# Entry products of a hybrid decoder block: where the weight sums are made, and when

## The chip, the cores and the metric

One Trainium2 chip, one of its cores. The metric is the device time of one execution in microseconds (us). A kernel is run several times and the median is given; one more execution is recorded by the hardware profiler, and all times of single instructions come from that one. TensorE (PE) multiplies matrices and loads their weights (PEld), VectorE (DVE) and ScalarE (ACT) work on elements, GpSimd (POOL) does so too and issues DMAs from its own queue, SyncE (SP) issues most DMAs. Each engine runs its instructions strictly in order.

## What is computed

A decoder block on one sequence of 1024 tokens with 1024 channels. The input is normed, scaled and shifted by a conditioning vector, which gives h. One large product `h @ w_in` yields the queries, keys, values and gates of a retention layer (4 heads), the queries, keys and values of dilated attention (3 groups of 4 heads), and two branch gates. The rest (retention by chunks of 128 tokens, attention, a squared-ReLU MLP) follows. Cut to what matters here:

```
h = modulate(rms_norm(x, g), sh1, sc1)
proj = h @ w_in
parts = jnp.split(proj, IN_OFFSETS, axis=-1)
rq, rk, rv, rg = parts[0], parts[1], parts[2], parts[3]
aq, ak, av = parts[4 + 3 * gi], parts[5 + 3 * gi], parts[6 + 3 * gi]
```

The change is in how the attention values `av` (and some of the retention values `rv`) are got from h. All operands and results are float32.

## The kernel before, in words

**Products.** Each float32 operand is split into a high and a low part, `hi` by a ScalarE cast and `lo` by a VectorE subtraction, and one product is three matmuls, `mm3` at L207 (low weights), L209 (low moving data) and L211 (both high); the names on a matmul line show what is multiplied. A block product of 2 x 2 blocks is done with seven block products in place of eight (a scheme of Strassen's kind). It needs sums of weight blocks, `s1` = 21 + 22, `s2` = s1 + 11, `s4` = s2 + 12 and `s3` = 21 + 11, where "21" names a block of the weight, and sums of blocks of h, called t1, t2, t3 and t4.

**Order.** The part around the change is written out by hand: the order in the program text is the order on each engine. Tiles come from pools with a few buffers per tag: `wraw` (three, for raw weights), `whl` (three each of "wh" and "wl"), `x4` (26, for anything of 128 x 1024). When a tile is placed in a buffer that an earlier tile used, its first instruction waits for the last use of that one. [...]

**Steps.** `first_values` (L800) makes plain values. `more_values` (L1012), called the entry below, runs eleven products i = 0 to 10 in the order of `USEQ`: four of the retention values (11, 11, 12, 12 for two halves), then seven of the attention values: 11, 12, s1, s2, s4, s3, 22. Each product has four parts p = 0 to 3 of twelve matmuls of 128 x 512, 48 in all, and its result is taken out of PSUM one part later by `u_post` (L956). `queries_keys` (L1209), called the pair stage, then runs 18 pairs of weight halves with the class `Blocks`, and after it `values` (L1329) makes the rest of the retention values. Then come the retention chunks, `chunk` (L690), and the rest of the block.

**Weights of the entry.** `u_load` (L911) loads the two raw tiles `ur` of product i from SP. For the products s1, s2 and s3 it loads block "21"; `u_add` (L924) then adds the other blocks by accumulating DMAs from POOL's queue (L931): one block on s1, two on s2, two more on s1's tile to make s4, one on s3, each for two tiles, 12 transfers in all of 512 KB. `u_w` (L933) makes `uwh` by ScalarE (L937) and queues the subtraction for `uwl` on VectorE (L940, L942). For product i + 1 it is called at p = 2 and 3 of product i. In between, an if/elif ladder places the scaling and splitting of h (`h_scale`, `h_split`) and its sums (`sums_of_h`, L1102).

**Around it.** `shift_out` (L1001) multiplies the plain values' correction, copies it to the tile `shw` and adds it to the stored values `vad` by four accumulating DMAs from POOL (L1010). `bias_out` (L445) stores three rows and spreads each by four broadcasts. `a_load` (L1145) loads the raw weights of a pair; those of pair 0 are loaded in product 9, those of pair 1 at the start of `queries_keys`. In `values`, `v_base` (L1321) loads the tile `vm` from DRAM and copies it into PSUM as the start value of `va`. At the end of `values`, three state tiles are made (L1367 to L1369), and with `chunk_tiles` before them they take over SBUF that the value products used. The first chunk's tile `sm` is written at L650, `state` at L737.

Of the kernel before, what the change touches and what calls it, by code (L numbers as in the profile page):

```python
# [11 lines left out]
F32 = mybir.dt.float32  # L12
# [5 lines left out]
P = 128  # L18
# [6 lines left out]
DV = 512  # L25
# [115 lines left out]
def block_kernel(ctx, tc, io, stop=None, dbg=None):  # L141
# [3 lines left out]
    def fv(t):  # L145
        return t.bitcast(F32)
# [246 lines left out]
    def bias_cut(t, g):  # L393

        return t[0][:, 384 * g:384 * g + 384] if g < 2 else t[1][:, :384]
# [42 lines left out]
    def bias_rows(g):  # L438
# [3 lines left out]
        r = bias_cut(rows, g)[:12]  # L442
        nc.scalar.copy(r, ps)

    def bias_out(g):  # L445

        nc.sync.dma_start(brow_d[g], bias_cut(rows, g)[:12])
# [459 lines left out]
    def u_block(i, blk, j):  # L907
        s, b = USEQ[i][0], ("11", "12", "21", "22").index(blk)
        return io["w_av2"][b, j] if s == "av" else io["w_rv"][b, 2 * int(s[1]) + j]

    def u_load(i):  # L911

        n = USEQ[i][1]
        for j in range(2):
            if i in (1, 7):
                t = x4(f"ur{i}{j}")
            elif i in (3, 5, 9):
                t = whl.tile([P, 1024], F32, tag=("wh", "wl")[j], name=f"ur{i}{j}")
            else:
                t = wraw.tile([P, 1024], F32, tag="raw", name=f"ur{i}{j}")  # L920
            U["raw", i, j] = t
            nc.sync.dma_start(t, u_block(i, "21" if n[0] == "s" else n, j))

    def u_add(i):  # L924

        n = USEQ[i][1]
        for blk in {"s1": ("22",), "s2": ("22", "11"), "s4": ("11", "12"), "s3": ("11",)}[n]:
            for j in range(2):
                if n == "s4":
                    U["raw", i, j] = U["raw", i - 2, j]  # L930
                nc.gpsimd.dma_start(U["raw", i, j], u_block(i, blk, j), accum_op=ALU.add, max_dma_last_dim=8192)  # L931

    def u_w(i, j):  # L933
# [3 lines left out]
        nc.scalar.activation(hi, src, AF.Copy, scale=sign)  # L937
        U["w", i, j] = hi, lo
        if sign > 0:
            late_low(lambda: nc.vector.tensor_sub(lo, src, fv(hi)))  # L940
        else:
            late_low(lambda: nc.vector.scalar_tensor_tensor(lo, src, -1.0, fv(hi), op0=ALU.mult, op1=ALU.subtract))  # L942
# [69 lines left out]
    def more_values(ahead):  # L1012

        last = len(USEQ) - 1
        post = []

        def ready(*fs):
            for f, *args in fs:
                f(*args)

        for i, (s, n) in enumerate(USEQ):
            if i in (0, 1, 2, 3, 8):
                u_load(i + 2)
            for k in {4: (6, 7), 5: (9,), 6: (8,)}.get(i, ()):
                if k != 8:
                    u_load(k)
                u_add(k)
            if i == 0:
                for m in range(4):
                    for p in range(4):  # L1030
                        u_mm(0, p, [m])
                u_w(1, 0)
                u_w(1, 1)
                for m in range(4):
                    shift_mod(2 * m + 1)
                late_low()
                for m in range(4):
                    shift_rows(2 * m)
                post = [(0, p) for p in range(4)]
                sh = mods[:, SH1:SH1 + NK].rearrange("p (m j) -> p m j", j=2)  # L1040
                nc.vector.tensor_sub(dsh1, sh[:, :, 0], sh[:, :, 1])
                continue
            for p in range(4):
                u_mm(i, p)
                while post:
                    u_post(*post.pop(0))
                post.append((i, p))
                if i == 1:
                    h_scale(2 * p + 1, 0)
                    h_split(2 * p + 1, 0)  # L1050
                elif i == 2:
                    h_scale(2 * p, 1)
                    shift_rows(2 * p + 1)
                elif i == 3:
                    sums_of_h("t1", [p])
                elif i == 4:
                    h_scale(2 * p + 1, 1)
                elif i == 5:
                    sums_of_h("t2", [p])
                elif i == 6:  # L1060
                    h_split(2 * p + 1, 1)
                    sums_of_h("t4s", [p])
                elif i == 7:
                    h_split(2 * p, 1)
                    sums_of_h("t3", [p - 1] if 0 < p < 3 else [2, 3] if p else [])
                elif i == 8:
                    if p == 0:
                        for m in range(4):
                            nc.sync.dma_start(h12_d[m][:, 0], fv(hh[2 * m][:, 512:]))
                            nc.sync.dma_start(h12_d[m][:, 1], fv(hl[2 * m][:, 512:]))  # L1070
                    if p > 0:
                        sums_of_h("t4", [p - 1])
                elif i == 9:
                    if p == 0:
                        sums_of_h("t4", [3])
                        nc.sync.dma_start(cs, io["cossin"])
                    if p == 1:
                        late_low()
                        a_load(0, 1)
                        a_load(0, 2)  # L1080
                elif i == last:
                    BA.prep((0, ORDER[p]))
                if i < last and p > 1:
                    u_w(i + 1, p - 2)
                    if p == 3:
                        late_low()
                if i == 2 and p == 3:
                    for g in range(3):
                        bias_out(g)
                if i == last and p == 0:  # L1090
                    shift_out()
        BA.flush()
        u_post(*post.pop())

# [112 lines left out]
    BA = Blocks("qa", XA, ["x"] * 4 + ["wh", "wl"] * 3, lambda kind: True, a_place, a_two, a_temps, a_out)  # L1207

    def queries_keys(ahead):  # L1209
        a_load(1, 1)  # L1210
        a_load(1, 2)
# [36 lines left out]

# [71 lines left out]

    def v_base(hp, p):  # L1321

        if p % 2 == 0:
            V["m", hp] = x4(f"vm{hp}{p}")
            nc.sync.dma_start(V["m", hp].rearrange("p (a b) -> p a b", a=2), m11_d[hp][:, p:p + 2])
        V["ps", "a", p] = ps_s(f"va{hp}{p}")
        nc.scalar.copy(V["ps", "a", p], V["m", hp][:, 512 * (p % 2):512 * (p % 2) + 512])

    def values(ahead):  # L1329
        last = len(VSEQ) - 1  # L1330
        for i, (hp, n) in enumerate(VSEQ):
            if i + 2 <= last:
                v_load(i + 2)
            for p in range(4):
                v_mm(i, p)
                if V["post"]:
                    v_post(*V["post"].pop())
                V["post"].append((i, p))
                if n == "s1" and p > 0:
                    v_base(hp, p - 1)  # L1340
                if n == "s2" and p == 0:
# [1452 lines left out]
```

## Time and profile before

| | us |
|---|---|
| runs | 2224.27, 2223.49, 2220.73 |
| median | 2223.49 |
| the profiled execution's own time | 2221.88 |
| its span, first to last instruction | 2220.1 |

TensorE's share of busy time is 98%, VectorE's 67%, ScalarE's 42%, POOL's 8%. The entry lies from 59 to 206 us, the pair stage behind it, the value products end near 671 us, and the first chunk follows.

How to read it. A timeline line has the start in us, the duration in us, the engine, the line of the kernel, the operation, output <- inputs, the shape, and in brackets the idle time of that engine just before and what ended it. Durations of matmuls overlap, so the time that one takes is the distance from its start to the next one's. In the view of waits each line has the waiting instruction, the one waited for, and the total, the number and the longest of the waits in us. A line for a stretch has its bounds, its length, the busy time of PE, PEld, DVE, ACT and POOL with the number of instructions, then the granted TensorE clock (1.00 is full speed), the share of the DMA engines and the GB/s moved. A group line ends with busy time in us and the mean duration in ns, then the idle time ahead of it and what ended it. A DMA line has the count, the size and the median time from issue to landing.

### The profile page before, as it was taken

To read this page: it belongs to the slowest core of one execution; us is meant where nothing else is said; L and a number is where in the kernel's file an instruction comes from. 1 tells how busy PE (TensorE), PEld (TensorE's weight loads), DVE (VectorE), ACT (ScalarE), POOL (GpSimd) and SP (SyncE) were. 2 spreads that over 40 slices of the span, in tenths; PEclk is the share of its full clock that TensorE was granted. 3 is DMA by queue.
4 is the path that set the end of the run, shared out by engine and by line. 5 is a ranking of instruction groups with operands and counts; after the bars stand their busy time and mean duration, and the time that the engine had idled before them with its cause. 6 is when DMAs were issued, how large, how long until landed. Compare 5 with 4: busy or idle time off the path is not lost. (4 is left out here: it accounts for less than half of the span.)

```text
span 2220.1 us, 27323 instructions
## 1 busy us (share of the span) xinstructions
PE 2170.3 (98%) x10084; PEld 1795.9 (81%) x10084; DVE 1484.3 (67%) x2325; ACT 943.3 (42%) x1730; POOL 175.5 (8%) x208
## 2 busy tenths in 40 slices
PE   8989999999999999999999999999999999999998
PEld 6767788888787888888888888888778888888887
DVE  6845777776456788764665654577886665887845
ACT  5533233222344445454654643434454445533413
POOL 0010111100011121111010000001100000000003
PEclk9999999999999999999999999999999999999999
DMA  9697999862676465547773256645144444745322
GB/s 384 208 271 228 289 293 291 216 190 99 235 253 237 160 204 196 176 151 217 186 200 98 80 208 214 244 162 177 47 158 155 156 157 157 272 140 172 123 86 76
DMA packets 161762, 419.93 MB, mean 189 GB/s; under 512 B 27861, under 2 KB 55772, under 8 KB 158556
## 3 DMA queue, kind: packets, MB, share of 16 engines
q1 hardware_dynamic: 150552, 365.52, 46.6%
q0 software_dynamic: 10752, 52.44, 11.2%
q8 instruction: 79, 1.29, 0.2%
q14 instruction: 55, 0.45, 0.1%
q10 hardware_dynamic: 324, 0.23, 0.0%
HBM read 323.08 MB, written 156.13 MB: 216 GB/s over the span
## 5 line engine op out<-in xcount | busy, mean ns | idle before, releaser
L207 PE MATMUL qap<-hh,qaw 128*128 128x512 f32 x216 | 84.9, 393 | 3.8 <-DVE qat L293 3.8
L209 PE MATMUL qap<-hl,qaw 128*128 128x512 f32 x216 | 84.6, 392 | 0.0
L211 PE MATMUL qap<-hh,qaw 128*128 128x512 f32 x216 | 84.5, 391 | 0.0
L615 POOL TENSOR_TENSOR j<-qk,j 128x512 fp32r<-128x512 f32 x32 | 43.2, 1351 | 426.0 <-ACT j L614 405.2
L2114 POOL TENSOR_TENSOR accnf<-accnf,sqnf 128x256 f32<-128x256 f32 (+1 forms) x18 | 16.6, 921 | 609.6 <-ACT sqnf L2110 609.6
L2218 ACT ACTIVATE a<-a 128x512 f32<-128x512 f32 x48 | 30.3, 632 | 73.6 <-DVE a L2217 73.6
L1534 ACT ACTIVATE P<-P,ng 128x128 f32<-128x128 f32 (+1 forms) x96 | 41.9, 438 | 37.1 <-DVE ng L1531 37.1
L264 DVE TENSOR_TENSOR fw<-w1r,fw 128x512 fp32r<-128x512 f32 x48 | 32.9, 688 | 33.6 <-ACT fw L254 33.6
L2426 ACT CAST w2h<-w2s 128x512 fp32r<-128x512 f32 x36 | 22.4, 621 | 77.4 <-DVE w2s L2464 74.5
L207 PEld LDWEIGHTS qap<-hh,qaw 128*128 128x128 f32 x216 | 40.9, 189 | 12.7 <-DVE qat L293 4.2
L207 PE MATMUL fp<-h2h,fw 128*128 128x512 f32 x128 | 50.0, 391 | 0.0
L211 PE MATMUL fp<-h2h,fw 128*128 128x512 f32 x128 | 49.8, 389 | 0.0
L650 ACT COPY sm<-sT 128x128 f32<-128x128 f32 x32 | 8.5, 267 | 97.1 <-PE sT L638 90.2
L207 PE MATMUL roa<-rh,rwl 128*128 128x512 f32 x128 | 49.8, 389 | 0.0
L209 PE MATMUL roa<-rl,rwh 128*128 128x512 f32 x128 | 49.8, 389 | 0.0
L211 PE MATMUL roa<-rh,rwh 128*128 128x512 f32 x128 | 49.8, 389 | 0.0
L209 PE MATMUL fp<-h2l,fw 128*128 128x512 f32 x128 | 49.8, 389 | 0.0
L1949 DVE TENSOR_TENSOR rwl<-rwl,rwh 128x1024 fp32r<-128x1024 f32 x25 | 30.2, 1221 | 29.0 <-ACT rwh L1979 29.0
L209 PEld LDWEIGHTS qap<-hl,qaw 128*128 128x128 f32 x216 | 41.0, 190 | 8.5
L211 PEld LDWEIGHTS qap<-hh,qaw 128*128 128x128 f32 x216 | 40.9, 189 | 8.6
L2114 POOL TENSOR_TENSOR accn<-accn,sqn 128x512 f32<-128x512 f32 x12 | 15.5, 1293 | 389.5 <-ACT sqn L2110 389.5
L2219 ACT ACTIVATE a<-a 128x512 f32<-128x512 f32 x64 | 40.5, 633 | 2.0
(3094 smaller groups left out, 7262.4 us busy)
## 6 DMA issues: line engine op xcount, KB each, us to landing
v<-vd SPq DMA_DIRECT2D x32, 512.0 KB, 6.7
raw<-in_w_ada_dram SPq DMA_DIRECT2D x32, 512.0 KB, 4.9
w1r<-in_w_ff_dram SPq DMA_DIRECT2D x32, 512.0 KB, 4.5
yt<-y POOLq DMA_DIRECT2D x24, 512.0 KB, 7.2
xsd<-as SPq DMA_DIRECT2D x24, 512.0 KB, 2.7
w2r<-in_w_ff2s_dram SPq DMA_DIRECT2D x24, 512.0 KB, 7.2
em<-in_w_ada_dram SPq DMA_DIRECT2D x16, 512.0 KB, 10.2
wrvs<-in_w_rv_dram POOLq DMA_DIRECT2D x16, 512.0 KB, 9.1
```

The source lines that it names most:

```text
L207: nc.tensor.matmul(o, wl, xh, start=first, stop=False, skip_group_check=skip)
L209: nc.tensor.matmul(o, wh, xl, start=False, stop=False, skip_group_check=skip)
L211: nc.tensor.matmul(o, wh, xh, start=False, stop=last, skip_group_check=skip)
L264: nc.vector.tensor_sub(t[:, 512:], src, fv(t[:, :512]))
L615: nc.gpsimd.tensor_sub(t[:, 1], src, fv(t[:, 0]))
L650: nc.scalar.copy(sm, ps[:, :C])
L1534: nc.scalar.activation(v, v, AF.Exp, bias=ng[:, blk:blk + 1], accum_out=st[:, g, blk, 2 + a:3 + a])
L1949: nc.vector.tensor_sub(lo, fv(lo), fv(hi))
L2114: (nc.vector if f == 7 else nc.gpsimd).tensor_add(G["acc", key], G["acc", key], sq)
L2218: nc.scalar.activation(o, o, AF.Relu)
L2219: nc.scalar.activation(o, o, AF.Square)
L2426: nc.scalar.copy(hi, src)
```

## The change

- *Sums of weights.* `u_add` and its 12 accumulating DMAs are gone. The tile `us`, loaded with "21" for s1 and for s3, holds a running sum; the next block comes into a tile `ur` by a plain load from SP, and `u_w` adds it on VectorE before the cast. There are 12 loads for the four sum products in place of 6, and eight new VectorE instructions of 128 x 1024.
- *Time of the weights.* `u_w` for part p of product i + 1 is called right after part p of product i, p = 0 and 1, in place of p = 2 and 3. `u_load` of i + 2 is called at p = 1 of product i from i = 4 on.
- *Table.* A table `work`, keyed by (i, p), says where each scaling, split and sum of h stands, in place of the ladder. Bias rows are stored at (1, 0) and spread at (2, 0) to (2, 2); both pairs' loads and the stores of `h12d` are in it, and the loads of pair 1 come ahead of `shift_out`.
- *Value products.* The tiles `vm` are loaded ahead by `v_base_load`: for the first half at the last pair's product 12, for the second at p = 0 of VSEQ 3.
- *State tiles.* They are made in the order low, high, state.

TensorE's instructions keep their order. On ScalarE the copy `qa` of pair 0's first output stands two instructions ahead of the first one that waited for the buffer of `shw`, and takes that buffer over.

```diff
-            if i in (1, 7):
+            if i == 1:
                 t = x4(f"ur{i}{j}")
-            elif i in (3, 5, 9):
+            elif n[0] == "s":
+                if n in ("s1", "s3"):
+                    U["sum", n, j] = t = wraw.tile([P, 1024], F32, tag="raw", name=f"us{i}{j}")
+                    nc.sync.dma_start(t, u_block(i, "21", j))
+                t = whl.tile([P, 1024], F32, tag=("wh", "wl")[j], name=f"ur{i}{j}")
+            elif i in (3, 5, 10):
                 t = whl.tile([P, 1024], F32, tag=("wh", "wl")[j], name=f"ur{i}{j}")
...
-            nc.sync.dma_start(t, u_block(i, "21" if n[0] == "s" else n, j))
-
-    def u_add(i):
+            nc.sync.dma_start(t, u_block(i, {"s1": "22", "s2": "11", "s4": "12", "s3": "11"}.get(n, n), j))
...
-                nc.gpsimd.dma_start(U["raw", i, j], u_block(i, blk, j), accum_op=ALU.add, max_dma_last_dim=8192)
...
-        sign, src = float(UPLAN[USEQ[i][1]][1]), U["raw", i, j]
+        sign, src = float(UPLAN[n][1]), U["raw", i, j]
+        if n[0] == "s":
+            t = U["sum", "s3" if n == "s3" else "s1", j]
+            nc.vector.tensor_add(t, t, src)
+            src = t
...
+        work = {
+            (1, 0): [(first_half, 1, 3), (rows_out,)], (1, 1): [(first_half, 5)], (1, 2): [(first_half, 7), (late_low,)],
+            (2, 0): [(scale, (0, 1)), (shift_rows, 1), (bias_out, 0)], (2, 1): [(scale, (2, 1)), (shift_rows, 3), (bias_out, 1)],
+            (2, 2): [(scale, (4, 1)), (shift_rows, 5), (sums_of_h, "t1", [0]), (bias_out, 2)],
+            (2, 3): [(scale, (6, 1)), (shift_rows, 7), (sums_of_h, "t1", [1])],
+            (3, 0): [(sums_of_h, "t1", [2])], (3, 1): [(sums_of_h, "t1", [3])], (3, 2): [(scale, (1, 1))],
+            (3, 3): [(scale, (3, 1))],
+            (4, 0): [(scale, (5, 1))], (4, 1): [(scale, (7, 1))], (4, 2): [(sums_of_h, "t2", [0])],
+            (4, 3): [(sums_of_h, "t2", [1])],
+            (5, 0): [(sums_of_h, "t2", [2])], (5, 1): [(sums_of_h, "t2", [3])], (5, 2): [(split, (1, 1), (3, 1))],
+            (5, 3): [(split, (5, 1), (7, 1))],
+            (6, 0): [(sums_of_h, "t4s", [0, 1])], (6, 1): [(sums_of_h, "t4s", [2, 3])],
+            (7, 0): [(split, (0, 1), (2, 1))], (7, 1): [(split, (4, 1), (6, 1))], (7, 2): [(sums_of_h, "t3", [0])],
+            (7, 3): [(sums_of_h, "t3", [1])],
+            (8, 0): [(sums_of_h, "t3", [2])], (8, 1): [(sums_of_h, "t3", [3]), (keep_12,)],
+            (9, 0): [(sums_of_h, "t4", [0, 1]), (nc.sync.dma_start, cs, io["cossin"])],
+            (9, 1): [(sums_of_h, "t4", [2, 3])], (9, 2): [(late_low,), (pair_load, 0)],
+            (10, 0): [(pair_load, 1), (shift_out,)],
+        }
+        for i in range(len(USEQ)):
+            if i < 4:
                 u_load(i + 2)
...
                 u_mm(i, p)
+                if p < 2 and i < last:
+                    u_w(i + 1, p)
                 while post:
                     u_post(*post.pop(0))
                 post.append((i, p))
...
-                if i < last and p > 1:
-                    u_w(i + 1, p - 2)
-                    if p == 3:
-                        late_low()
...
+                if p == 1 and 3 < i <= last - 2:
+                    u_load(i + 2)
+                for f, *args in work.get((i, p), ()):
+                    f(*args)
+                if i == last:
                     BA.prep((0, ORDER[p]))
...
+            if q == NA - 1 and n == "12":
+                v_base_load(0)
...
-        if p % 2 == 0:
-            V["m", hp] = x4(f"vm{hp}{p}")
-            nc.sync.dma_start(V["m", hp].rearrange("p (a b) -> p a b", a=2), m11_d[hp][:, p:p + 2])
         V["ps", "a", p] = ps_s(f"va{hp}{p}")
-        nc.scalar.copy(V["ps", "a", p], V["m", hp][:, 512 * (p % 2):512 * (p % 2) + 512])
+        nc.scalar.copy(V["ps", "a", p], V["m", hp, p // 2][:, 512 * (p % 2):512 * (p % 2) + 512])
+
+    def v_base_load(hp):
+
+        for j in range(2):
+            V["m", hp, j] = t = x4(f"vm{hp}{j}")
+            nc.sync.dma_start(t.rearrange("p (a b) -> p a b", a=2), m11_d[hp][:, 2 * j:2 * j + 2])
...
+                if i == 3 and p == 0:
+                    v_base_load(1)
...
+        R["sl"] = R["p"].tile([P, 2, DV], F32R, name="statel")
+        R["sh"] = R["p"].tile([P, 2, DV], F32R, name="stateh")
         R["state"] = R["p"].tile([P, 2, DV], F32, name="state")
-        R["sh"] = R["p"].tile([P, 2, DV], F32R, name="stateh")
-        R["sl"] = R["p"].tile([P, 2, DV], F32R, name="statel")
```

More of the change, by code (lines that the diff above doesn't have):

```diff
@@ L443, in bias_rows, with bias_row_out @@
         nc.scalar.copy(r, ps)
+    def bias_row_out(g):
+        nc.sync.dma_start(brow_d[g], bias_cut(rows, g)[:12])
     def bias_out(g):
-        nc.sync.dma_start(brow_d[g], bias_cut(rows, g)[:12])
         for a in range(4):
@@ L1014, in more_values, with scale, split, first_half @@
         last = len(USEQ) - 1
[L1015 to L1022, printed above, removed]
+        def scale(*tiles):
+            for k, j in tiles:
+                h_scale(k, j)
+        def split(*tiles):
+            for k, j in tiles:
+                h_split(k, j)
+        def first_half(*ks):
+            for k in ks:
+                h_scale(k, 0)
+                h_split(k, 0)
@@ new lines, in keep_12, with rows_out, pair_load @@
+        def keep_12():
+            for m in range(4):
+                nc.sync.dma_start(h12_d[m][:, 0], fv(hh[2 * m][:, 512:]))
+                nc.sync.dma_start(h12_d[m][:, 1], fv(hl[2 * m][:, 512:]))
+        def rows_out():
+            for g in range(3):
+                bias_row_out(g)
+        def pair_load(q):
+            for part in (1, 2):
+                a_load(q, part)
+        work = {
[17 more added lines that the diff above has]
+        }
@@ L1038, in more_values @@
                     shift_rows(2 * m)
-                post = [(0, p) for p in range(4)]
                 sh = mods[:, SH1:SH1 + NK].rearrange("p (m j) -> p m j", j=2)
                 nc.vector.tensor_sub(dsh1, sh[:, :, 0], sh[:, :, 1])
+                post = [(0, p) for p in range(4)]
                 continue
@@ L1047, in more_values @@
                 post.append((i, p))
[L1048 to L1077, printed above, removed]
-                        late_low()
-                        a_load(0, 1)
-                        a_load(0, 2)
-                elif i == last:
-                    BA.prep((0, ORDER[p]))
-                if i < last and p > 1:
-                    u_w(i + 1, p - 2)
-                    if p == 3:
[L1086 to L1091, printed above, removed]
+                if p == 1 and 3 < i <= last - 2:
[3 more added lines that the diff above has]
+                if i == last:
+                    BA.prep((0, ORDER[p]))
+                if p == 3:
+                    late_low()
         BA.flush()
```

12 lines of the change are left out of this document (1 added, 11 removed).

## Prediction

> **What bounds the kernel now.** I read the page first, then the waits of TensorE over the whole span, then the waits, stretches and timelines of the stage that the diff rewrites.
>
> ```profile
> span 2220.1 us, 27323 instructions
> PE 2170.3 (98%) x10084; PEld 1795.9 (81%) x10084; DVE 1484.3 (67%) x2325; ACT 943.3 (42%) x1730; POOL 175.5 (8%) x208
> ```
>
> TensorE is busy for 98% of the span, so a change that leaves its matmuls alone can only win the time in which it stands or runs at a low clock. Its longest waits (total, times, longest):
>
> ```profile
> PE uavc L207 <- ACT uwh L937: 9.4, 3, 4.8
> ...
> PE qap L207 <- DVE qat L293: 3.8, 1, 3.8
> PE kv L207 <- DVE kl L664: 3.8, 2, 3.1
> ...
> PE uavc L209 <- DVE uwl L940: 1.9, 4, 0.5
> ...
> PE va L207 <- ACT va L1327: 1.5, 1, 1.5
> ```
>
> The first and fourth lie in the entry products, the others where the change moves a load or a tile. What ScalarE's cast `uwh` itself waits for, and what POOL waits for, in 59 to 210 us:
>
> ```profile
> POOL ur L931 <- DMA ur<-in_w_av_dram: 93.2, 6, 78.1
> ...
> ACT uwh L937 <- DMA ur<-in_w_av_dram: 21.3, 6, 7.1
> ```
>
> So the chain is: accumulating DMA lands, ScalarE casts, VectorE subtracts, TensorE starts. [...] The stretches (length, PE, PEld, DVE, ACT, POOL busy, TensorE clock, DMA share, GB/s):
>
> ```profile
> 59.10:206.30 147.20, 131.92 (x531) 102.30 (x530) 91.87 (x129) 60.40 (x91) 11.97 (x13) 0.93 0.76 226
> 134.60:142.44 7.84, 6.91 (x14) 4.48 (x15) 5.61 (x7) 2.60 (x4) 0.88 (x1) 0.51 1.06 248
> 166.27:176.50 10.23, 8.02 (x17) 5.19 (x17) 6.49 (x8) 7.25 (x11) 0.00 (x0) 0.51 0.81 266
> ```
>
> The second and third follow a stall each, and the clock in them is half. The matmuls around:
>
> ```profile
> 110.26 0.39 PE L211 MATMUL uava<-uwh,hh 128*128 128x512 f32 x1
> ...
> 117.06 0.39 PE L211 MATMUL uava<-uwh,hh 128*128 128x512 f32 x1
> ...
> 129.40 0.39 PE L211 MATMUL uavb<-uwh,hh 128*128 128x512 f32 x1
> 134.60 0.80 PE L207 MATMUL uavc<-uwh,xat 128*128 128x512 f32 x1 [4.81 <-ACT uwh L937]
> ...
> 142.44 0.39 PE L211 MATMUL uavc<-uwh,xat 128*128 128x512 f32 x1
> ...
> 162.59 0.39 PE L211 MATMUL uava<-uwh,xat 128*128 128x512 f32 x1
> 166.27 0.79 PE L207 MATMUL uavc<-uwh,hl 128*128 128x512 f32 x1 [3.29 <-ACT uwh L937]
> ...
> 176.50 0.39 PE L209 MATMUL uavc<-uwl,hh 128*128 128x512 f32 x1
> ```
>
> From 110.26 to 117.06 lie 30 steps of one matmul, 0.2267 us each: the pace without stalls. From 129.40 to 142.44 lie 15 steps, 13.04 us where 3.40 were needed: 9.64 lost. From 162.59 to 176.50, 17 steps, 13.91 for 3.86: 10.05 lost. The idle time itself is 4.81 and 3.29; the rest is half clock and the smaller waits after it.
>
> **The change part by part.**
>
> *Entry stalls.* The stage has 11 products of 48 matmuls, 528 in all: 528 x 0.2268 = 119.75 us. It takes 147.20, so 27.4 are lost. About 0.9 of this is the product `shw`, and 0.8 are waits at 62 and 72 us, ahead of what is reordered. Recoverable are 25.7, of which 19.7 are the two stalls above and the rest some ten waits of 0.2 to 1.2 us for `uwl` at the starts of products. Now every weight of product i+1 is made at p = 0 and 1 of product i, half a product (5.4 us) earlier, and the sums come from plain loads.
>
> What this costs is VectorE: two adds of 128x1024 in each of four products. Its nearest row is the subtraction of the same size and operands:
>
> ```profile
> L940 DVE TENSOR_TENSOR uwl<-ur,uwh 128x1024 fp32r<-128x1024 f32 x14 | 17.0, 1223 | 21.1 <-ACT uwh L937 20.7 <-DMA vd<-uor 0.3
> ```
>
> Eight adds at 1.22 are 9.8, so VectorE has 91.9 + 9.8 = 101.7 us of work in a stage of about 121: it fits on average. By the table, products 2 and 5 hold some 12.2 and 12.6 us of it against a product's 10.9, the others 8 to 11.2. The surplus, 1.5 each, is mostly splits that nobody needs at once, so I take 1.5 us of stall left in all (bounds 0 and 4).
>
> *The loads.* SP issues six more, POOL twelve fewer.
>
> ```profile
> DMA to landing us min/median/max: 3.9/7.6/16.1
> ```
>
> ```profile
> ur<-in_w_av_dram SPq DMA_DIRECT2D x12, 512.0 KB, 10.1
> ```
>
> The first line is for tile `ur` in 59 to 200 us, the second for its loads by SP. Each sum product's second operand goes through one slot: the load for product i+2 is issued when VectorE has added that of i+1, at p = 1 of product i. So one turn takes a landing T, the add (1.22), the issue (0.33) and some 0.3 of handover: T + 1.9. This is under a product's 10.9 us for T below 9.0, and four products in a row lose 4(T - 9.0) above. At T = 3.9 nothing, at 10.1 4.4 us, at 16.1 28.4. I take about 4.5, near the lowest: the 10.1 was seen while accumulating DMAs ran in the same stretches, and those are gone, 12 of them for 6 loads. From this part: -25.7 + 1.5 = **-24.2**, bounds -25.7 and 0.
>
> [...]
>
> *The start of the pair stage.* Here ScalarE waits for the transfers of `shw` to have read its tile, and TensorE stops behind it:
>
> ```profile
> 206.46 0.39 PE L207 MATMUL qap<-hh,qaw 128*128 128x512 f32 x1
> ...
> 244.80 0.80 PE L207 MATMUL qap<-hh,qaw 128*128 128x512 f32 x1 [3.79 <-DVE qat L293]
> ```
>
> On ScalarE and on POOL's queue:
>
> ```profile
> 222.09 0.59 ACT L1177 ACTIVATE qa<-qap 128x512 f32<-128x512 f32 x1
> ...
> 233.85 0.62 ACT L254 CAST qaw1s<-qas 128x512 fp32r<-128x512 f32 x1 [9.68 <-DMA vad<-shw]
> ```
>
> ```profile
> 226.24 1.22 POOL L1010 DMA_DIRECT2D vad<-shw  x1 [11.74 <-issue]
> ```
>
> Call the stage's start E (206.4). The last of the four transfers is issued at E + 19.9 and has landed at L = E + 27.5. TensorE loses 7.3 us: 1.7 at 235 and 5.6 at 244.8 with the slow stretch behind it. In the changed order the first instruction that needs this slot stands two earlier on ScalarE: the copy `qa`, at E + 15.8 by its row. Then the matmul of 244.80, which followed L by 10.9, comes behind 3.4 more (two ScalarE and three VectorE operations of 0.6 to 0.7): it starts at L + 14.4, or at E + 32.6 if nothing waits. Loss: (L - 18.2) + 1.6 of slow clock (eight steps of 0.43 in place of 0.23, as behind the idle 4.81 and 3.29 above). The loads of pair 1, two of 0.5 MB, are now issued before `shw` instead of beside its transfers; at the 266 GB/s of the third stretch above they took 3.9 us of it, so I take L = 24 and a loss of 7.4: **0**. With L unchanged at 27.5 it is +3.6; with L below 20, -4.
>
> *The base of the value products.* `va` now finds its tile loaded many products earlier.
>
> ```profile
> 567.17 0.39 PE L211 MATMUL vc<-vwh,xat 128*128 128x512 f32 x1
> 569.05 0.50 PE L207 MATMUL va<-vwh,xat 128*128 128x512 f32 x1 [1.49 <-ACT va L1327]
> ```
>
> The step of 1.88 loses 1.65, and the matmuls right behind another 0.7: **-2.4** (bounds 0 and -2.4: the subtraction of `vwlTrue` may still be late).
>
> *The order of the state tiles.* The tile `sm` of the first chunk lies today where a row `vr` is being stored, and waits for it:
>
> ```profile
> 675.62 0.61 PE L211 MATMUL rg<-hh,raw_4756h 128*128 128x512 f32 x2
> 679.35 0.50 PE L207 MATMUL kv<-v,kl 128*128 128x512 f32 x1 [3.12 <-DVE kl L664]
> ```
>
> ```profile
> 677.16 0.27 ACT L650 COPY sm<-sT 128x128 f32<-128x128 f32 x1 [6.98 <-DMA vd<-vr]
> ```
>
> The stores, and the landing of a row `vr` in 655 to 690 us (least, median, most):
>
> ```profile
> 663.26 8.00 SPq L1319 DMA_DIRECT2D vd<-vr  x4
> ```
>
> ```profile
> DMA to landing us min/median/max: 9.8/10.7/11.6
> ```
>
> The step of 3.73 loses 3.3; a later wait for the copy of `state` loses 0.6. With the new order `sm` waits only for TensorE, but `state` and `bn` take the place of the last stored `vr`. That store is issued at 670.9 (0.3 before the end of its group) and lands about 681.6, 0.4 to 1.3 after the copy of `state` is due. Behind that copy on ScalarE stand the casts for the next chunk. 3.9 lost today, 1.9 then: **-2.0** (0 to -3.5).
>
> *The rest.* The spread of h's sums, the bias broadcasts and the `h12d` stores move on engines with room; TensorE's order is untouched. On SP the broadcasts now follow their row stores by a product and need not wait for them; behind the moved stores and pair loads stand stores of results, which nobody awaits. 0, as VectorE's slack hides it; without that it is in the 4 us above.
>
> Sum: -24.2 + 0 - 2.4 - 2.0 = -28.6. The profiled execution took 2221.88 (span 2220.1 and 1.8 around it): 2193.3. The median shown, 2223.49, is 1.6 above that run: **2195**.
>
> **The rivals.**
> 1. *Loads land late.* The stall moves from the accumulating DMA to the chain load, add, cast, subtract, at T about 10: 4.4 more, less what the 1.5 already holds: 2198 to 2200. For it: the median of 10.1. Against it: the accumulating half of the transfers goes. [...]
> 2. *The pair stage pays.* L stays at 27.5 or later, because POOL's transfers still share with the SP loads behind E: 2199 at 27.5, 2203 at E + 32. For it: the wait stands two instructions ahead on ScalarE.
> 3. *VectorE becomes the bound of the entry.* If the in-order queue holds weights behind the h sums, each of eight products loses 1 us or so, 8 less the 1.5 already allowed: 2201. For it: 101.7 of 121 us. Against it: most of what stands in products 2 and 5 is due later.
> 4. *The one slot (slower).* The load of the next operand waits in SP's queue behind a store that waits for VectorE, and VectorE's add waits for that load. Place: products 6 to 9. Price: 4(T - 9.0). The gain without it is 25.7 + 4.4 = 30.1, so it decides from T = 16.5; slower by 0.2% needs 17.6, and at T = 18.5 the time is 2223.5 + 38.0 - 30.1 = 2231. For it: one landing of 16.1. Against it: all four turns need it.
> 5. *The change does not do what it says*: the two long stalls have another cause than the sums. The releaser rows speak against it (7.1 us for `ur` before the very cast): 2223.5, within 0.2%.
>
> **How the numbers follow.** Forecast 0.64 (2190 to 2198), rivals 1 to 3 together 0.27 (2198 to 2208), rival 4 0.06, rival 5 0.03. The lower end has every term at its good bound: 25.7 + 4 + 2.4 + 3.5 = 35.6, which gives 2188 at the median; I take 2187. The upper end is rival 1 with rival 2 at E + 32: 2195 + 4.4 + 8.1 = 2208. A measurement here can tell about 0.2%, 4.4 us: faster 0.91, same 0.03, slower 0.06.
>
> **What would show it.** In the profile after: no wait of `uavc` for `uwh` above 1 us, no POOL rows of `ur`, the first `qap` near 182 with the clock at 1.00 through the entry (right for the first term); landings of `ur` under 9 (the second); ScalarE's long wait for `vad<-shw` on `qa` and not on `qaw1s`, ending about 24 us after the first `qap`; no wait of `va`; `sm` released by TensorE and `state` by `vd<-vr`. The prediction is wrong if `uwh` or the adds wait for `ur` by several us in products 6 to 9, or if the wait on `shw` ends beyond E + 30.

## The result and the profile after

The changed kernel takes 2194.98 us in the median of four runs (2193.72 to 2195.34). Four runs of the kernel before, beside it, have a median of 2223.88. The ratio is 0.9869, with a 95% interval of 0.9852 to 0.9886: 1.3% less, 28.9 us. The profiled execution took 2194.82 us. Its page starts so:

```profile
span 2193.0 us, 27323 instructions
## 1 busy us (share of the span) xinstructions
PE 2160.1 (98%) x10084; PEld 1794.8 (82%) x10084; DVE 1492.3 (68%) x2333; ACT 942.8 (43%) x1730; POOL 165.0 (8%) x196
```

The number of TensorE's instructions is the same. VectorE has eight more (the adds) and POOL twelve fewer (the accumulating DMAs). The busy share of TensorE, 98%, does not tell that anything happened; the waits do. TensorE's waits over the whole span of the changed kernel:

```profile
PE qap L207 <- DVE qaw1s L264: 5.6, 1, 5.6
...
PE qap L207 <- DVE qat L293: 2.4, 1, 2.4
...
PE kv L207 <- ACT state L739: 1.0, 1, 1.0
...
PE kv L207 <- DVE statel L721: 0.7, 1, 0.7
```

The waits of `uavc` for `uwh` and `uwl` are gone, and so is that of `va`. The first line is new, and larger than what stood at that place. The entry as one stretch (columns as before):

```profile
58.79:180.27 121.48, 121.23 (x531) 99.33 (x530) 100.00 (x137) 60.07 (x91) 1.43 (x1) 1.00 0.74 257
```

It is 121.48 us long in place of 147.36 (from the first `ur0a` to the first `qap`), TensorE is busy in all but 0.25 us of it, and the clock is 1.00 throughout. VectorE works 100.00 us, near the 101.7 that was added up. Its adds and the casts behind them, by line in 58 to 181 us:

```profile
L937 DVE TENSOR_TENSOR us<-us,ur 128x1024 f32<-128x1024 f32 x8 | 9.8, 1219 | 0.4 <-DMA ur<-in_w_av_dram 0.4
L940 ACT ACTIVATE uwh<-us 128x1024 fp32r<-128x1024 f32 x8 | 8.5, 1062 | 15.5 <-DVE us L937 15.5
```

The adds took 1219 ns each and waited 0.4 us for their loads, all eight together. For the loads of `ur` in the entry the DMA view now gives a median of 4.4 us from issue to landing, where it gave 10.1:

```profile
ur<-in_w_av_dram SPq DMA_DIRECT2D x14, 512.0 KB, 4.4
```

These two medians do not compare like with like, because the profile tells the landing of only three of these loads in either kernel. Before, they were issued at 109.58, 115.04 and 116.27 us and took 6.7, 10.1 and 10.5, and all three were issued ahead of the first accumulating DMA (124.55). After, two were issued at 82.90 and 83.37, well ahead of the sum products, and one at 137.82; they took 4.4, 5.2 and 4.3. What accumulating DMAs cost the plain loads beside them is therefore not shown.

Behind the entry, on TensorE, ScalarE and POOL:

```profile
180.27 0.39 PE L207 MATMUL qap<-hh,qaw 128*128 128x512 f32 x1
...
204.53 0.39 PE L211 MATMUL qap<-xat,qaw1s 128*128 128x512 f32 x1
210.55 0.80 PE L207 MATMUL qap<-xat,qaw1s 128*128 128x512 f32 x1 [5.64 <-DVE qaw1s L264]
...
223.04 0.50 PE L207 MATMUL qap<-hh,qaw 128*128 128x512 f32 x1 [2.40 <-DVE qat L293]
```

```profile
208.67 0.60 ACT L1182 ACTIVATE qa<-qap 128x512 f32<-128x512 f32 x1 [12.72 <-DMA vad<-shw]
```

```profile
173.68 1.43 POOL L1013 DMA_DIRECT2D vad<-shw  x1 [127.31 <-DMA vad<-ur]
181.02 1.24 POOL L1013 DMA_DIRECT2D vad<-shw  x1 [5.91 <-issue]
193.22 1.21 POOL L1013 DMA_DIRECT2D vad<-shw  x1 [10.97 <-issue]
202.52 1.22 POOL L1013 DMA_DIRECT2D vad<-shw  x1 [8.09 <-issue]
```

Each of the four transfers was issued about 0.3 us after the one before it had landed; they took 7.1, 11.9, 9.0 and 6.0 us. The copy `qa` stands on ScalarE for 12.72 us until the last transfer of `shw` has read its tile, at 208.67 = E + 28.4. The matmul at 223.04 is the 145th of the pair stage (the product 22 of pair 1), which was at 244.80 = E + 38.3 before and is at E + 42.8 now.

To see where the 27.1 us of span went, I cut both traces at the same matmuls:

| stage | before | after | difference |
|---|---|---|---|
| up to the first matmul of the entry | 59.10 | 58.79 | -0.3 |
| entry, to the first `qap` (E) | 147.36 | 121.48 | -25.9 |
| E to the 145th matmul of the pair stage | 38.34 | 42.77 | +4.4 |
| from there to the first `va` | 324.25 | 322.76 | -1.5 |
| first `va` to the first `rg` | 99.53 | 97.92 | -1.6 |
| first `rg` to the ninth `sT` (first chunk) | 18.72 | 16.46 | -2.3 |
| rest | 1532.80 | 1532.82 | 0.0 |

### The profile page after: what moved, and what is told of

It is laid out like the page before. It is cut to its first block, busy times and chain, and to the rows that moved or that the text cites. A ratio compares the mean times of both kernels' runs of the same rounds, so it can differ in the third digit from the quotient of the medians.

```text
span 2193.0 us, 27323 instructions
## 1 busy us (share of the span) xinstructions
PE 2160.1 (98%) x10084; PEld 1794.8 (82%) x10084; DVE 1492.3 (68%) x2333; ACT 942.8 (43%) x1730; POOL 165.0 (8%) x196
## 5 line engine op out<-in xcount | busy, mean ns | idle before, releaser
L2124 POOL TENSOR_TENSOR accnf<-accnf,sqnf 128x256 f32<-128x256 f32 (+1 forms) x18 | 16.6, 921 | 609.6 <-ACT sqnf L2120 609.6
L2228 ACT ACTIVATE a<-a 128x512 f32<-128x512 f32 x48 | 30.3, 631 | 73.7 <-DVE a L2227 73.7
L207 PEld LDWEIGHTS qap<-hh,qaw 128*128 128x128 f32 x216 | 40.8, 189 | 11.3 <-DVE qat L293 2.8
L1949 ACT ACTIVATE rh<-rl 128x512 fp32r<-128x512 f32 x56 | 31.7, 625 | 23.4 <-PE roc L209 8.4
```

Of the source, the lines that this page charges most:

```text
L207: nc.tensor.matmul(o, wl, xh, start=first, stop=False, skip_group_check=skip)
L1949: nc.scalar.activation(hi, fv(lo), AF.Copy, scale=sign)
L2124: (nc.vector if f == 7 else nc.gpsimd).tensor_add(G["acc", key], G["acc", key], sq)
L2228: nc.scalar.activation(o, o, AF.Relu)
```

## The experiments

The theory behind the forecast has three parts. The entry's stalls came from the chain accumulating DMA, cast, subtraction. The pair stage's loss comes from the wait for the transfers of `shw`. The value products and the first chunk lost to one late load and one buffer. Against each stood a rival. The stages of all runs, cut as above (us):

| run | entry | E to 145th | 145th to `va` | `va` to `rg` | `rg` to `sT` | rest | time |
|---|---|---|---|---|---|---|---|
| before | 147.4 | 38.3 | 324.3 | 99.5 | 18.7 | 1532.8 | 2223.9 |
| after | 121.5 | 42.8 | 322.8 | 97.9 | 16.5 | 1532.8 | 2195.0 |
| own tile for `shw` | 121.4 | 32.6 | 321.0 | 97.9 | 15.9 | 1533.9 | 2183.9 |
| `shift_out` earlier | 121.5 | 44.1 | 321.0 | 97.9 | 15.9 | 1532.8 | 2194.2 |
| pair 1's loads back | 121.5 | 38.3 | 323.9 | 97.9 | 21.5 | 1533.4 | 2197.4 |
| sums by DMA | 130.7 | 38.9 | 322.7 | 97.9 | 16.5 | 1533.0 | 2200.2 |
| weights late | 132.8 | 39.7 | 321.1 | 97.9 | 18.4 | 1531.4 | 2202.4 |
| `vm`, state back | 121.4 | 43.5 | 323.0 | 99.6 | 18.9 | 1533.3 | 2200.1 |
| loads three times | 145.4 | 43.0 | 322.7 | 97.9 | 15.9 | 1534.9 | 2221.3 |
| before, own tile | 149.6 | 32.6 | 323.0 | 100.2 | 15.7 | 1534.8 | 2216.7 |
| state copies first | 121.4 | 32.7 | 321.0 | 97.9 | 15.7 | 1535.7 | 2184.4 |

The rest of the kernel, which no run touches, differs by up to 4.3 us between them, so differences of a stage are read from the stage and not from the time.

**An own tile for `shw`.**

```diff
-        t = x4("shw")
-        for j in range(2):
-            nc.scalar.copy(t[:, 512 * j:512 * j + 512], ps)
+        t = xpool.tile([P, 1, 512], F32, tag="shw", bufs=1, name="shw")
+        nc.scalar.copy(t[:, 0], ps)
...
-            nc.gpsimd.dma_start(dst, t.rearrange("p (a x) -> p a x", a=2), accum_op=ALU.add)
+            nc.gpsimd.dma_start(dst, t.to_broadcast([P, 2, 512]), accum_op=ALU.add)
```

> The changed kernel with the 128x512 result of shift_out in a tile of its own of 2 KB a partition, read twice by each accumulating DMA; nothing else moved. Theory (the copy qa waits until the four transfers have read the tile, and all of the pair stage's loss hangs on that wait): no wait of qa for vad<-shw, the step of 5.64 us idle at 210.55 and the one of 2.40 at 223.04 both gone, the matmul now at E + 42.8 back at E + 32.6 to 33, time 2195.0 - 10 to 11.7 = 2183.3 to 2185. Rival (the weights of pair 1 or VectorE's backlog are late anyway, and the wait only covers it): most of the idle time stays, 2191 to 2195.

Measured: 2183.85 us (2181.84 to 2184.22), ratio to the kernel before 0.9828 (0.9811 to 0.9844). TensorE's waits from 59 to 235 us, all of them, and the stage's first and 145th matmul:

```profile
PE ur1a L209 <- DVE uwl L943: 0.2, 1, 0.2
```

```profile
180.89 0.39 PE L207 MATMUL qap<-hh,qaw 128*128 128x512 f32 x1
...
213.53 0.39 PE L207 MATMUL qap<-hh,qaw 128*128 128x512 f32 x1
```

213.53 is E + 32.6, where a matmul stands for which nothing waits. POOL's last transfer was issued even later than in the changed kernel:

```profile
204.93 1.22 POOL L1012 DMA_DIRECT2D vad<-shw  x1 [8.52 <-issue]
```

So it is not the transfers but the buffer that cost: 42.8 - 32.6 = 10.1 us there and 1.8 behind it. The theory holds, and the rival falls. This is the fastest version found.

**`shift_out` one product earlier.**

```diff
-            (9, 0): [(sums_of_h, "t4", [0, 1]), (nc.sync.dma_start, cs, io["cossin"])],
+            (9, 0): [(shift_out,), (sums_of_h, "t4", [0, 1]), (nc.sync.dma_start, cs, io["cossin"])],
...
-            (10, 0): [(pair_load, 1), (shift_out,)],
+            (10, 0): [(pair_load, 1)],
```

> The changed kernel with shift_out called at the start of product 9 in place of product 10, one product (10.9 us) earlier, with the tile still in the shared pool. Theory: L falls from E + 28.4 to about E + 17.5; the first instruction that then needs the buffer is VectorE's subtraction for the output qa, due at E + 12.5, so VectorE stands some 5 us, but TensorE needs the next sums only from E + 19 on: loss 0 to 2, time 2183.5 to 2186. Rival (the transfers slow down when they lie beside the loads and stores of product 9 and 10, and land no earlier than E + 24): loss 4 to 7, time 2188 to 2191. Rival of e2 (the wait only covers other lateness): 2191 to 2195.

Measured: 2194.18 us (2193.12 to 2194.67), no gain; 44.1 us to the 145th matmul, a loss of 11.5. E is 180.65; VectorE and TensorE behind it:

```profile
204.80 0.69 DVE L1184 TENSOR_TENSOR qa<-qat,qap 128x512 f32<-128x512 f32 x1 [11.65 <-DMA vad<-shw]
```

```profile
206.14 0.79 PE L207 MATMUL qap<-hh,qaw0s 128*128 128x512 f32 x1 [9.01 <-DVE qaw0s L264]
```

The transfers were called one product (10.9 us) earlier and landed only 4.3 earlier, at E + 24.2. They took 9.2, 10.5, 13.3 and 7.7 us, 40.6 in all in place of 34.0. Why they took longer beside the loads and stores of products 9 and 10 is not shown. And the buffer now went to an output that VectorE writes at E + 12.5, so all of VectorE stood 11.65 us. The first rival was right on the landing, E + 24; its loss of 4 to 7 was too low, as TensorE lost nearly all of the time that VectorE stood. An earlier start buys little if a still earlier instruction inherits the buffer.

**The loads of pair 1 back at the start of the pair stage.**

```diff
     def queries_keys(ahead):
+        a_load(1, 1)
+        a_load(1, 2)
...
-            (10, 0): [(pair_load, 1), (shift_out,)],
+            (10, 0): [(shift_out,)],
```

> The changed kernel with the loads of pair 1 back at the start of the pair stage, as in the kernel before. The prediction's step (these loads beside the transfers of shw cost 3.9 us of L): L grows from E + 28.4 to about E + 32, time 2198 to 2199. Rival (L is set by POOL's own handing out, one transfer after the other, and by the other copies that SP issues at the start of the stage): L within 1.5 us of E + 28.4, time 2194 to 2196.5, or the weights of pair 1 late by themselves.

Measured: 2197.38 us, one run. On ScalarE, where the transfers' end is seen, and on TensorE:

```profile
209.10 1.14 ACT L254 CAST qaw<-wa 128x512 fp32r<-128x512 f32 x2 [7.95 <-DMA vad<-shw]
...
649.66 0.27 ACT L652 COPY sm<-sT 128x128 f32<-128x128 f32 x1 [7.41 <-DMA vd<-vr]
```

```profile
218.85 0.79 PE L207 MATMUL qap<-hh,qaw 128*128 128x512 f32 x1 [5.05 <-DVE qat L293]
...
652.63 0.79 PE L207 MATMUL kv<-v,kl 128*128 128x512 f32 x1 [4.32 <-DVE kl L666]
```

L is 209.10 - 180.57 = E + 28.5, the same as with the loads moved: the 3.9 us that the prediction gave to these loads are not there, and the rival holds for L. From the first issue on POOL to the end of the wait it is 35.1 us here (from 173.98) and 35.0 in the changed kernel (from 173.68); in the kernel before, with these loads beside the transfers, it was 33.9 (199.97 to 233.85). The time falls between the two ranges, because two other things happened that no expectation had. The buffer of `shw` went to an instruction later in ScalarE's order, so up to the 145th matmul the pair stage lost 4.5 us less. And the rotation of the buffers, shifted by the same move, put `sm` of the first chunk under a stored `vr` again, as in the kernel before, for 5.1 us more there.

**Sums by accumulating DMAs again**, with the early weights and the table kept: `u_load`, `u_add` and their calls as before.

```diff
-            if i < 4:
+            if i in (0, 1, 2, 3, 8):
                 u_load(i + 2)
+            for k in {4: (6, 7), 5: (9,), 6: (8,)}.get(i, ()):
+                if k != 8:
+                    u_load(k)
+                u_add(k)
...
-                if p == 1 and 3 < i <= last - 2:
-                    u_load(i + 2)
```

> The changed kernel with the weight sums made by the 12 accumulating DMAs from POOL again, loads and adds placed as in the kernel before; weights are still made at p = 0 and 1, and the rest is as changed. Theory (the chain of accumulating DMAs set the two long stalls): the sums land when they did, the stalls at the first and third sum product are back with 9 to 10 us each and perhaps more, since the cast now stands earlier in ScalarE's order and blocks what is behind it: entry 140 to 147 us in place of 121.5, time 2214 to 2221. Rival (the half product of lead won most of it, and the sums by VectorE matter little): entry under 127 us, time under 2201.

Measured: 2200.23 us, one run; entry 130.7. TensorE's waits in 58 to 230 us for the weights, and POOL's first three accumulating DMAs:

```profile
PE uavc L207 <- ACT uwh L939: 3.6, 1, 3.6
...
PE uava L207 <- ACT uwh L939: 1.0, 1, 1.0
```

```profile
111.69 3.05 POOL L933 DMA_DIRECT2D ur<-in_w_av_dram  x3 [65.04 <-DMA ur<-in_w_av_dram]
```

The kernel before had its first ones here:

```profile
124.55 2.03 POOL L931 DMA_DIRECT2D ur<-in_w_av_dram  x2 [78.12 <-DMA ur<-in_w_av_dram]
```

Only one of the two long stalls is left. My expectation was wrong, and the rival too, though it was nearer: the entry gave back 9.2 of the 25.9 us. The accumulating DMAs start at 111.7 in place of 124.6, because SP issued the loads of the block to which they add at 104.45 and 104.95 in place of 113.63 and 115.04. In the kernel before these two loads waited for no raw tile. They stood in SP's order behind the broadcasts of the bias rows, which waited for the rows to be stored (SP's waits in the kernel before, 59 to 210 us):

```profile
SPq L450 <- DMA browd<-rows: 5.1, 2, 3.2
SPq L450 <- DMA browd<-onehot: 3.3, 1, 3.3
```

The table `work` stores the rows a product earlier, and in this run the broadcasts wait 2.0 us in all in place of 8.4. So what this run keeps of the gain, 16.7 us, belongs to the early weights and this table together.

**Weights late again**, with VectorE's sums.

```diff
-                if p < 2 and i < last:
-                    u_w(i + 1, p)
...
-                if p == 1 and 3 < i <= last - 2:
-                    u_load(i + 2)
...
+                if i < last and p > 1:
+                    u_w(i + 1, p - 2)
                 if p == 3:
                     late_low()
+                    if 3 < i <= last - 2:
+                        u_load(i + 2)
```

> The changed kernel with the weights of product i + 1 made at p = 2 and 3 of product i again, and the loads for product i + 2 (from i = 4 on) called behind them at p = 3; sums by VectorE as in the change. The run with accumulating DMAs and early weights gave back 9.2 of the 25.9 us that the entry had won. Theory (the half product of lead won more than the sums by VectorE): without it each of the four sum products starts 2 to 2.5 us late (add 1.2, cast 1.1, subtraction 1.2 behind the last part), the others about 1: entry 128 to 137 us in place of 121.5. Rival (the two halves of the change are worth little alone, and VectorE's sums are enough): entry under 126.

Measured: 2202.43 us, one run; entry 132.8, in the range of the theory, but only in part at the places that it named. The longest wait for `uwl`, 3.6 us, is in a retention product, where nothing is summed:

```profile
PE ur1a L209 <- DVE uwl L943: 3.8, 2, 3.6
...
PE uavc L209 <- DVE uwl L943: 1.5, 2, 0.8
PE uavc L207 <- ACT uwh L940: 1.5, 1, 1.5
```

That product took 16.6 us (93.4 to 110.0) in place of 10.9, half of the 11.3 us that the entry gave back; the four sum products gave back 4.5 together.

So the half product of lead with the table `work` wins 16.7 us of the entry (sums by DMA: 147.4 to 130.7), VectorE's sums with the table 14.6 (147.4 to 132.8), and all three 25.9. The two add up to 5.4 more than the whole. No run has the lead or the sums without the table, so it stays open whether the two shorten the same stalls or whether the 5.4 are the table's own gain, counted twice.

**Each load of a sum product's operand three times.**

```diff
+        for j in (0, 1, 0, 1) if n[0] == "s" else ():
+            nc.sync.dma_start(U["raw", i, j], u_block(i, {"s1": "22", "s2": "11", "s4": "12", "s3": "11"}[n], j))
```

> The changed kernel with each load of a second operand of a sum product issued three times into the same tile, each behind the one before, so that it takes three landings; 16 transfers of 512 KB more. The landing T becomes 11 to 14 us in place of 4.4. The prediction's rule for the one slot, 4(T - 9.0): 8 to 20 us lost, time 2203 to 2215. Rival (the casts and subtractions have slack of a product or more, so that T up to 14 is hidden): under 3 us lost, time under 2198. A second rival (SP's queue, blocked by the second and third landing, delays the stores and pair loads behind it): more than 20.

Measured: 2221.25 us, one run; entry 145.4, 23.9 us lost: above the 8 to 20 of the rule, and in the range of the second rival. Four adds of the first halves on VectorE, and its longest wait in 100 to 200 us:

```profile
122.87 1.23 DVE L939 TENSOR_TENSOR us<-us,ur 128x1024 f32<-128x1024 f32 x1 [8.54 <-DMA ur<-in_w_av_dram]
...
140.92 1.23 DVE L939 TENSOR_TENSOR us<-us,ur 128x1024 f32<-128x1024 f32 x1 [5.82 <-DMA ur<-in_w_av_dram]
...
155.79 1.23 DVE L939 TENSOR_TENSOR us<-us,ur 128x1024 f32<-128x1024 f32 x1 [6.68 <-DMA ur<-in_w_av_dram]
...
171.87 1.23 DVE L939 TENSOR_TENSOR us<-us,ur 128x1024 f32<-128x1024 f32 x1 [4.17 <-DMA ur<-in_w_av_dram]
```

```profile
DVE us L939 <- DMA ur<-in_w_av_dram: 25.4, 5, 8.5
```

The adds come 18.1, 14.9 and 16.1 us apart, 16.3 in the mean, where the changed kernel has a product's 10.9. The loads were called at 129.25, 143.14 and 157.05 on SP, so a threefold load took 11.7, 12.7 and 14.8 until its add, 13.0 in the mean. A turn is then T + 3.3 in the mean, not T + 1.9. From the start of an add to the call of the next load it took 6.4, 2.2 and 1.3 us: in the first turn SP stands behind a store (`vad<-ur`, issued at 128.88) that waits for VectorE. Three turns that are 5.4 too long, and a first add that comes 8.1 us later after the start of the entry than in the changed kernel, make 24.3, near the 23.9 lost. TensorE's longest wait in 100 to 206 us is not for weights. VectorE, standing at the adds, is late in taking outputs out of PSUM:

```profile
PE uavc L207 <- DVE ur L993: 6.7, 2, 3.8
```

The rival of hidden slack falls. The second rival has the number, but its cause, stores and pair loads held up behind the landings, is not what these rows show. The rule has the right form, and its point of decision lies nearer than I had it.

**The tiles `vm` and the state tiles as before.** The second half of the edit puts the three state tiles back in the order state, high, low.

```diff
     def v_base(hp, p):
+        if p % 2 == 0:
+            V["m", hp, p // 2] = t = x4(f"vm{hp}{p}")
+            nc.sync.dma_start(t.rearrange("p (a b) -> p a b", a=2), m11_d[hp][:, p:p + 2])
...
-            if q == NA - 1 and n == "12":
-                v_base_load(0)
...
-                if i == 3 and p == 0:
-                    v_base_load(1)
```

> The changed kernel with the tiles vm loaded where they are used and the state tiles in the old order: two separate stages in one run. Theory (each won what the two profiles show): from the first matmul of va to the first of rg 97.9 + 1.6 = 99.5 us and a step of about 1.9 ahead of va, from the first rg to the ninth sT 16.5 + 2.3 = 18.7 us, time 2195 + 5 to 6 = 2200 to 2201. Rival (the buffers fall in another order behind the other edits, so that the old code finds no store in its way): one of the two stages stays as it is in the changed kernel.

Measured: 2200.12 us, one run; 99.6 and 18.9 us in the two stages. TensorE's waits in 530 to 680 us:

```profile
PE kv L207 <- DVE kl L666: 2.9, 2, 2.3
PE va L207 <- ACT va L1330: 1.7, 1, 1.7
```

Both waits of the kernel before are back, and both stages have their old length: these two edits won what the table of stages gives them. Both were put back in one run, so that each acts in its own stage alone is argued from the places of the two waits.

**The kernel before with nothing but the own tile.** The edit is that of the first experiment.

> The kernel before with nothing changed but the tile of shw, which gets its own 2 KB a partition. Theory (the wait for the transfers of shw made the whole of the 7.3 us lost there too): the step of 1.8 at 233 and the one at 244.8 with its slow stretch are gone, the 145th matmul of the pair stage at E + 32.6 in place of E + 38.3, and the entry stays at 147: 2223 - 7.3 = 2215 to 2217. Rival (VectorE's backlog in the older order is late by itself): E + 35 or more, 2218 to 2221.

Measured: 2216.67 us, one run. E is 208.56, and the 145th matmul:

```profile
241.19 0.39 PE L207 MATMUL qap<-hh,qaw 128*128 128x512 f32 x1
```

E + 32.6 here too: the wait for `shw` made the whole loss at this place in both kernels. The time agrees with the expectation partly by chance, as the entry was 2.2 longer and the first chunk 3.0 shorter, probably because the later tiles got other buffers; the cause of the longer entry was not looked for.

**The copies of `state` first**, on the own tile.

```diff
         if g == 0:
+            for i in range(2):
+                nc.scalar.copy(st[:, i, :], kvs[i])
             jit_qk(2)
         ahead(2)
...
-        for i in range(2) if g == 0 else ():
-            nc.scalar.copy(st[:, i, :], kvs[i])
```

> The changed kernel with the own tile for shw, and in the first chunk the two copies of state ahead of ScalarE's cast for the third chunk's j, which waited for a load. What is left at the first chunk in the run with the own tile is one idle step of 0.97 us for the copy of state. Theory (the copy stands behind that cast, not behind the stored vr): the step goes, from the first rg to the ninth sT 15.9 - 0.9 = 15.0 us, time 2183. Rival (the prediction's: state waits for the last stored vr): the copy waits for vd<-vr at its new place and the stage keeps 15.9 us or more, time 2184.

Measured: 2184.36 us (2182.93 to 2184.97), no difference that can be told from the own tile alone; the stage 15.7 in place of 15.9. ScalarE and TensorE:

```profile
643.88 1.19 ACT L729 COPY state<-kv 128x512 f32<-128x512 f32 x2 [0.27 <-DVE statel L721]
```

```profile
644.40 0.47 PE L207 MATMUL kv<-v,kl 128*128 128x512 f32 x1 [1.09 <-DMA v<-vd]
```

The copies wait for no store, as the theory has it, but the gain went to the next thing in line: TensorE now waits 1.09 us for the load of the chunk's values.

## Why the prediction came out

The forecast for the median, 2195, was met to a tenth of a microsecond. This is more than its working deserves: against the profiled execution it had 2193.3, and that took 2194.8; and the steps erred to both sides.

- *Entry, -24.2 forecast, -25.9 measured.* The stall left over, taken as 1.5, was 0.25: TensorE did not wait for the surplus of VectorE in products 2 and 5. VectorE's work was taken as 101.7 and was 100.0. T was taken as 4.5; the one load of the slot whose landing the profile tells took 4.3, and the only one that an add waited for took 5.9. But the reason given for T was a misreading: the 10.1 is the median of three loads that were issued before any accumulating DMA, and the 16.1 is a store of `ur` to `vad` (issued at 127.82), not a load. The forecast's words put 19.7 of 25.7 on the accumulating DMAs. With these DMAs back only 9.2 were lost again, so most of their stalls go with the early weights and the table `work`. Its move of the bias rows, which took 6.4 us of waiting off SP ahead of the loads, had been put at 0.
- *Pair stage, 0 forecast, +4.4 measured: the step that failed.* Its mechanism and its rule were right: the 145th matmul starts at L + 14.4 (28.4 + 14.4 = 42.8), and without the wait at E + 32.6. Wrong was L = 24. The loads of pair 1 beside the transfers cost L nothing; with them moved or not it is E + 28.4 and 28.5. This is rival 2, near the price that it gave for an unchanged L (3.6); its cause, that the transfers share with SP's loads behind E, is not shown.
- *Value products, -2.4 forecast.* The wait of 1.65 ahead of `va` went, and 1.6 more between `va` and `rg`: -3.1 in the two stages that hold them. In the changed kernel the first `va` follows at the pace:

```profile
545.57 0.39 PE L211 MATMUL vc<-vwh,xat 128*128 128x512 f32 x1
545.80 0.39 PE L207 MATMUL va<-vwh,xat 128*128 128x512 f32 x1
```

- *First chunk, -2.0 forecast, -2.3 measured, partly for another reason.* `sm` no longer waits for a store, as said. But what is left is not the last stored `vr`. ScalarE in the changed kernel:

```profile
647.04 0.27 ACT L652 COPY sm<-sT 128x128 f32<-128x128 f32 x1 [1.73 <-PE sT L640]
...
656.85 0.62 ACT L616 CAST j<-qk 128x512 fp32r<-128x512 f32 x1 [1.09 <-DMA qk<-qkd]
657.38 1.07 ACT L739 COPY state<-kv 128x512 f32<-128x512 f32 x2
```

`state` follows a cast that waited for the load of `qk`. The stores of `vr` landed after 8.6 to 10.0 us and were done by then, so the wait that I had put there cost nothing.
- *The rest, 0 forecast, 0.0 measured* in the profiled execution.
- *The slower rival* (one slot for the loads) did not decide: the eight adds waited 0.4 us in all. With T + 3.3 for a turn, an estimate from the run with the threefold loads, loss starts at T = 10.9 - 3.3 = 7.6 and not at 9.0, so the change has less margin than the prediction gave it.

Not settled: why the four transfers of `shw`, 512 KB each, take 6 to 13 us, and why they go one after the other; the profile says only "issue" for the time between them.

## What to carry to other kernels

A tile that a slow transfer still reads costs not where it is made but where its buffer is inherited (here 10.1 us up to the 145th matmul): look up which instruction gets it next, and on which engine, before moving anything by a product. Any added, removed or moved tile turns the rotation for all that follow, so a stage far from the edit can change (the first chunk from 16.5 to 21.5 us with pair 1's loads back); compare stage by stage. When two runs each take back one half of a change, whatever both keep, here the table `work`, is counted in both, so their parts need not add up to the whole. Before a median of landings is read, look how many landings it holds, and when those transfers were issued.

## What was not expected of the hardware

- The four accumulating DMAs of `shw` ran one at a time: in the kernel before, in the changed kernel and in the runs with the own tile, `shift_out` earlier or pair 1's loads back, each was issued 0.26 to 0.35 us after the one before it had landed. Three accumulating DMAs on `ur` were in flight together in the kernel before (issued at 124.55, 125.72 and 127.02; the first landed at 133.41). What makes the difference is open.
- The granted clock fell after less idle time than in the kernel before. There the stretches at 0.50 or 0.51 in the entry and the pair stage (134.60 to 142.44, 166.27 to 176.50, 244.80 to 247.95) stood behind idle times of 4.81, 3.29 and 3.79 us. In the changed kernel TensorE stood for 2.40 us, ran on at 0.23 to 0.34 us for five matmuls, and then took 0.43 for seven, at a granted clock of 0.50 from 224.36 to 227.40:

```profile
223.04 0.50 PE L207 MATMUL qap<-hh,qaw 128*128 128x512 f32 x1 [2.40 <-DVE qat L293]
...
224.36 0.63 PE L211 MATMUL qap<-hh,qaw 128*128 128x512 f32 x1
224.79 0.63 PE L207 MATMUL qap<-hh,qaw 128*128 128x512 f32 x1
```

The idle 3.12 us ahead of 679.35 in the kernel before had no such stretch behind it: the granted clock was 1.00 from there to 685.00. So in these two kernels the length of one idle time alone does not tell whether the clock falls. What decides it is not shown.
